# A two-layer decoder trunk on eight cores: the sample group transposed, its outer products in two row tiles, gMLP weights loaded transposed in bf16, first loads in turn

## The chip, the cores and the metric

The kernel runs on all 8 cores of one Trainium2 chip. Each core computes one prompt sequence of 2048 tokens and 16 of the 128 single-token samples; the cores do not exchange data. The metric is device time in microseconds (us) of the slowest core. Most executions agree closely: 17 of the 20 runs of the kernel before took 1262.70 to 1264.68 us. Some fall into a second, slower state: two or four cores of one die (four of the eight) show a lower granted clock (the share of TensorE's full clock that the trace records), and the time is longer.

PE is TensorE, DVE is VectorE, ACT is ScalarE, POOL is GpSimd, SP is SyncE, which here only issues DMA transfers.

## The reference, cut

```python
D_MODEL, BATCH, SEQ, DEPTH, DEC_BATCH, DEC_SEQ = 1024, 8, 2048, 2, 128, 1
# 8 retention heads and 8 gMLP heads of width 128, chunks of 128 tokens

def _layer(h, pos, S0, norm_g, w_in, w_out, ws, bs, ln_g, ln_b):
    xn = _rmsnorm(h, norm_g)
    q, k, v, g_r, u, v_g, g_g = split(xn @ w_in)            # 7 x 1024 columns
    q, k = rope(q), rope(k) * 128 ** -0.5
    o, S = _retention(q, k, v, S0)         # S_n = g S_{n-1} + k_n^T v_n ; o_n = q_n S_n
    o = o * rsqrt(mean(o * o) + EPS) * silu(g_r)            # per head
    vn = _layernorm(v_g, ln_g, ln_b)
    s = _spatial_gate(vn, ws, bs)          # s_i = sum_{j<=i} W[i,j] v_j + b_i, lower triangle
    m = u * s * silu(g_g)
    return h + concat(o, m) @ w_out, S, vn

def reference(...):
    for l in range(DEPTH):                 # prompt and sample share the weights
        h_p, S_p, _   = _layer(h_p, pos_p, zeros, ...)
        h_s, S_s, v_s = _layer(h_s, pos_s, state_ret[l], ...)
    return _rmsnorm(h_p), _rmsnorm(h_s), states_prompt, states_sample, vn_sample
```

For a sample of one token, the state update is one outer product of k and v per sample and head, and the spatial gate needs only the first element of each head's weight and bias.

## The kernel before

A list scheduler takes each operation with its reads, writes and an estimated duration, and orders the instructions of every engine. A layer runs in three stages: the v and v-gate projections of 16 chunks ("V stage"), 32 units of 8 heads and 4 token groups ("head stage"), and the output projection of 16 chunks ("out stage"). The sample's work is threaded through them.

The sample has its 16 rows on 16 partitions; its activations are the stationary operand, and the weights stream past, 512 columns at a time:

```python
        s_at = cur[0]
        stt = [T("stt%d" % i, [128, 8, 128], F32) for i in range(2)]     # sample states, 2 halves of 8
        ...
        xh_s = T("xh_s", [NS, D], F32, at=s_at)       # these five lie ON the state tiles
        lng_s = T("lng_s", [NS, D], F32, at=s_at + 4096)
        hs = T("hs", [NS, D], F32, at=s_at)           # (lnb_s, xs_s, fing_s cut)
        ...
        def s_mm(i):
            b = tbank()
            def mm(e):
                for k in range(8):
                    r = e.matmul(ps[0:NS, b, :], sxT[:, k, :], wv[i][:, k, :], start=(k == 0), stop=(k == 7))
                return r
            pe(mm, sxT.k() + wv[i].k(), [bk(b)], 8 * MM)
            return b
        ...
        def sample_vg(l, after=()):                   # LayerNorm of the sample's v-gate
            b0 = s_mm(2)
            b1 = s_mm(3)
            i = ln_stats(NS, b0, b1)
            # ... ACT normalises into xh_s; POOL: xh_s *= lng_s; POOL: xh_s += lnb_s (1024 columns each)
            pe(tr, xh_s.k() + identf.k(), [bk(b)], 8 * SM)      # 8 fp32 transposes
            # ... DVE: two passes into sT_s
        ...
        def w_prep(l, h):                             # gMLP weights: transpose, mask, sum of columns
            b = brot()
            pe(lambda e: e.transpose(ps[:, b, 0:128], ws_h[:], identf[:]), ws_h.k() + identf.k(), [bk(b)], 0.25)
            dve(lambda e: e.tensor_tensor(out=WTf[:], in0=ps[:, b, 0:128], in1=maskT[:], op=ALU.mult), ...)
            pool(lambda e: e.tensor_copy(WT[h % 2][:], WTf[:]), WTf.k(), WT[h % 2].k(), 128)
        def w_prep2(l, h):
            pe(lambda e: e.matmul(ps[:, b2, 0:128], ones_f[:], WTf[:], start=True, stop=True), ...)   # fp32
        ...
        def s_kv(l, h, half):                         # outer products k^T v of 8 samples, 4 to a matmul
            t = stt[half]
            for j in range(2):
                b = brot()
                pe((... e.matmul(ps[:, b, :], kn_s[:], vmask[:, j * 4:j * 4 + 4, :]...)), ..., [bk(b)], MM)
                # ... DVE: t = gamma * t + ps
```

`vmask` holds v of each sample in its own block of 128 columns and zero elsewhere, so one matmul with 16 rows makes four outer products. The first loads and the start of layer 0:

```python
        def x_load(l, c):
            xi[c] = dma("sp", hb[c % 4][:], src[c * 128:(c + 1) * 128, :], ...)     # a chunk of x, 512 KB
        ...
        for c in range(4):
            x_load(0, c)
            if c == 0:
                ld(identf, c_ident)
                ld(small, c_small, 51200)
                dma("sp", hs[:], xs_in, ...)
                w_item(0, ("v", 0))                   # first v weight: two loads on POOL's queue
        for l in range(DEPTH):
            if l == 0:
                for c in range(4):
                    norm_front(c); x_load(0, c + 4); norm_back(0, c, 1 + (c == 0))
                for n, (i, k) in enumerate(((1, 0), (1, 4), (2, 0), (2, 4), (3, 0), (3, 4))):
                    w_item(0, ("v", i, k), after=[xi[n + 2]])
                sample_norm(0)
            ...                                       # the V stage
            for half in range(2):
                s_load(l, 0, half)                    # states of head 0: stt[half], 512 KB each, on SP
```

## Time and profile before

| | before |
|---|---|
| time, median of 20 runs (fast about 1263) | 1263.73 us |
| mean granted TensorE clock, by core | 0.993 to 0.994 |
| PE busy | 1217.7 us, 96% |

The first lines are from the page of the kernel before, the profile of its slowest core: busy time, share of the span and number of instructions of each engine; then the engines' shares of the chain of work that ended last.

```profile
PE 1217.7 (96%) x7666; PEld 610.2 (48%) x7666; DVE 735.0 (58%) x1443; ACT 611.7 (48%) x1020; POOL 539.3 (43%) x536
...
PE 92%; DVE 3%; issue 2%; ACT 1%; DMA 1%; POOL 1%; SPq 0%; DVEq 0%; ACTq 0%; POOLq 0%
```

PE is busy almost throughout and is 92% of the chain. From this I expected that PE time taken away in a dense stretch comes off the total one for one (e13 below tests it), and that the other engines matter only where PE waits for them.

The next lines are the timeline of PE on core 3: start, duration, engine, line, output and inputs, partitions x columns, count; in brackets the idle time before and what ended it. Consecutive matmuls overlap in this view (a single one of 512 columns shows 0.379 us, yet eight take 1.73 from start to start), so costs are read from start to start.

```profile
8.29 1.01 PE L530 MATMUL ps<-identb,xs_105 128*128 128x128 bf16 x8 [8.29 <-DVE xs_105 L514]
...
19.95 1.01 PE L530 MATMUL ps<-identb,xs_106 128*128 128x128 bf16 x8 [4.97 <-DVE xs_106 L514]
...
33.34 1.89 PE L563 MATMUL ps<-wv_102,xnT 128*128 128x512 bf16 x8
...
57.06 1.89 PE L604 MATMUL ps<-wv_101,sxT 128*16 128x512 bf16 x8
58.79 1.89 PE L604 MATMUL ps<-wv_102,sxT 128*16 128x512 bf16 x8
60.61 1.90 PE L563 MATMUL ps<-wv_103,xnT 128*128 128x512 bf16 x8
...
103.11 5.30 PE L563 MATMUL ps<-wv_101,xnT 128*128 128x512 bf16 x16 [3.66 <-ACT VM L451]
...
191.01 0.60 PE L897 MATMUL ps<-vmask,kn_s 16*128 16x512 bf16 x2
191.54 0.49 PE L839 MATMUL ps<-WTf,ones_f 128*128 128x128 f32 x2
191.86 1.89 PE L658 MATMUL ps<-xnT,wsl_54 128*128 128x512 bf16 x8
...
229.12 1.89 PE L658 MATMUL ps<-xnT,wsl_61 128*128 128x512 bf16 x8
230.84 0.22 PE L773 MATMUL ps<-scT_89,VO 128*128 128x128 bf16 x1
```

First: transposes start at 8.29, but chunk 1's only at 19.95, and the second v weight (wv_102) is used at 33.34. Then the sample's v projection: 16 wide matmuls, 57.06 to 60.61, 3.55 us. At 103.11 PE had idled for 3.66 us, and the 16 matmuls that follow take 5.1 us instead of 3.5. Next, a pair of outer products takes 191.01 to 191.54, 0.53 us, and the fp32 column sum 0.32. The last two lines are eight projection matmuls, 1.72 us from start to start.

The issues of SP's queue on core 3 (SPq: start, time the queue was held, destination and source): chunks 0, 1, 2 and, once its normalisation frees a buffer, chunk 4.

```profile
1.06 0.38 SPq L461 DMA_DIRECT2D hb_50<-xp  x1
...
2.90 0.42 SPq L461 DMA_DIRECT2D hb_51<-xp  x1
3.37 0.95 SPq L461 DMA_DIRECT2D hb_52<-xp  x1
...
8.22 0.33 SPq L461 DMA_DIRECT2D hb_50<-xp  x1
```

And the timeline of DVE on core 3 just before the last two PE lines above. Note the order: the masking of the scores (scT, which PE's line 773 needs) runs ahead of the two B_k passes of the rotary embedding.

```profile
228.03 0.68 DVE L667 TENSOR_TENSOR A_k<-ps,rope_48 128x512 f32<-128x512 f32 x1
228.64 0.74 DVE L733 SCALAR_TENSOR_TENSOR scT_89<-ps,small,maskT 128x512 bf16<-128x512 f32 x1
229.41 0.69 DVE L671 TENSOR_TENSOR B_k<-ps,rope_48 64x512 f32<-64x512 f32 x1
230.11 0.68 DVE L672 TENSOR_TENSOR B_k<-ps,rope_48 64x512 f32<-64x512 f32 x1
```

The table below splits the time into stages, from starts in the PE timeline, mean of the eight cores of the profiled run: start of the program to the sample's v projection; the rest of layer 0's V stage; and so on; the last stage ends with the last matmul.

| us | start to sample v | rest of V, layer 0 | heads 0 | out 0 | V, layer 1 | heads 1 | out 1 |
|---|---|---|---|---|---|---|---|
| before | 56.7 | 102.2 | 360.2 | 127.9 | 120.4 | 364.1 | 120.4 |

### The profile page before, as it was taken

The numbers are of one execution on the slowest core, as the hardware profiler recorded it, in microseconds if no ns is written. First come the engines' busy times: TensorE is split into PE (matmuls) and PEld (weight loads), VectorE is DVE, ScalarE is ACT, GpSimd is POOL, SyncE is SP. The second block draws the span as 40 slices with busy tenths as digits, with TensorE's granted clock in tenths as the row PEclk, the third lists the DMA queues.
The fourth block names the chain that finished last, engine by engine and source line by source line (L and its number), as shares of the span: only waits on it lengthen the run. The fifth ranks groups of instructions, "written<-read, shape, count | busy, mean of one in ns | idle before, by whom it ended". The sixth has DMA issues, their size and how long they took to land.

```text
span 1262.4 us, 23383 instructions; the slowest of 8 cores (1258.4 to 1262.4 us)
## 1 busy us (share of the span) xinstructions
PE 1217.7 (96%) x7666; PEld 610.2 (48%) x7666; DVE 735.0 (58%) x1443; ACT 611.7 (48%) x1020; POOL 539.3 (43%) x536
## 2 busy tenths in 40 slices
PE   3998999999999999999999999999999999999997
PEld 1444455555555555444444444555555555544443
DVE  3464467776776767453443334776777767763333
ACT  3353346556566665422222434566665665753222
POOL 1002137667666766400000312667766766750000
PEclk9999999999999999999999999999999999999999
DMA  9726406225424523547650260325424523444433
GB/s 194 191 78 130 67 6 116 57 64 116 90 49 92 114 57 91 124 166 203 142 168 0 63 109 5 71 57 111 97 48 93 107 55 72 120 111 130 150 120 117
DMA packets 105687, 124.65 MB, mean 99 GB/s; under 512 B 5664, under 2 KB 79648, under 8 KB 105568
## 3 DMA queue, kind: packets, MB, share of 16 engines
q1 hardware_dynamic: 89440, 85.40, 22.3%
q0 software_dynamic: 16128, 37.76, 19.2%
q8 instruction: 64, 1.05, 0.3%
q14 instruction: 55, 0.45, 0.1%
HBM read 126.01 MB, written 34.87 MB: 127 GB/s over the span
## 4 chain that ended last, share of the span: by engine, by line
PE 92%; DVE 3%; issue 2%; ACT 1%; DMA 1%; POOL 1%; SPq 0%; DVEq 0%; ACTq 0%; POOLq 0%
PE ps L658 43%; PE ps L938 19%; PE ps L563 15%; PE ps L897 1%; PE ps L728 1%; PE ps L792 1%; PE ps L857 1%; PE ps L812 1%; PE ps L746 1%; PE ps L604 1%; PE ps L773 1%; PE ps L715 1%; DMA hb_51<-xp 1%; PE ps L776 1%; PE ps L530 1%
## 5 line engine op out<-in xcount | busy, mean ns | idle before, releaser
L451 ACT ACTIVATE B_q<-ps 64x512 f32<-64x512 f32 x128 | 75.8, 592 | 65.8 <-DVE A_q L683 57.7
L451 ACT ACT_TABLE_LOAD x65 | 83.4, 1283 | 48.4 <-DVE tt L794 46.4
L787 POOL TENSOR_TENSOR VO<-og,tt 128x512 bf16<-128x512 f32 x64 | 80.1, 1274 | 31.2 <-ACT tt L451 31.1
L674 POOL TENSOR_TENSOR kT_84<-A_k,B_k 128x512 bf16<-128x512 f32 x32 | 40.7, 1271 | 84.1 <-DVE B_k L672 84.1
L563 PE MATMUL ps<-wv_101,xnT 128*128 128x512 bf16 x256 | 62.4, 398 | 11.8 <-DVE xnT L535 7.8
L755 DVE SCALAR_TENSOR_TENSOR S_90<-S_90,ps 128x128 f32<-128x128 f32 x240 | 67.6, 282 | 6.9 <-PE ps L746 2.6
L451 ACT ACTIVATE tt<-tt 128x1024 f32<-128x1024 f32 x64 | 67.4, 1053 | 2.3 <-ACT tt L451 0.4
L889 POOL TENSOR_TENSOR vmask<-eye_137,v_s 16x1024 bf16<-16x1024 f32 x32 | 60.4, 1887 | 10.4 <-PE ps L897 9.8
L563 PE MATMUL ps<-wv_104,xnT 128*128 128x512 bf16 x256 | 61.1, 379 | 0.0
L563 PE MATMUL ps<-wv_103,xnT 128*128 128x512 bf16 x256 | 60.9, 379 | 0.2 <-ACT VM L451 0.2
L563 PE MATMUL ps<-wv_102,xnT 128*128 128x512 bf16 x256 | 57.4, 379 | 0.0
L576 DVE CAST VO<-ps 128x512 bf16<-128x512 f32 x32 | 21.8, 690 | 56.5 <-PE ps L563 56.5
L782 DVE TENSOR_TENSOR og<-ps,sgr_96 128x512 f32<-128x512 f32 x32 | 22.1, 691 | 53.2 <-ACT sq L451 53.2
L822 POOL TENSOR_TENSOR VM<-s_100,sgg_99 128x512 bf16<-128x512 f32 x32 | 36.9, 1153 | 37.1 <-DVE s_100 L816 30.5
L623 POOL TENSOR_TENSOR xh_s<-xh_s,lng_s 16x1024 f32<-16x1024 f32 x2 | 4.7, 2338 | 107.5 <-ACT xh_s L451 107.5
L451 ACT ACTIVATE sq<-ps 128x512 fp32r<-128x512 f32 x64 | 38.2, 597 | 24.9 <-PE ps L776 24.1
L782 DVE TENSOR_TENSOR og<-ps,sgr_97 128x512 f32<-128x512 f32 x32 | 22.1, 692 | 48.1 <-ACT sq L451 48.1
L535 DVE TENSOR_TENSOR xnT<-ps,small 128x1024 bf16<-128x1024 bf16 (+1 forms) x33 | 39.0, 1183 | 17.1 <-PE ps L530 12.4
L563 PEld LDWEIGHTS ps<-wv_101,xnT 128*128 128x128 bf16 x256 | 25.4, 101 | 43.5 <-issue 18.2
L674 POOL TENSOR_TENSOR kT_85<-A_k,B_k 128x512 bf16<-128x512 f32 x32 | 40.8, 1274 | 12.8 <-DVE B_k L672 12.7
L688 POOL TENSOR_TENSOR qT_82<-A_q,B_q 128x512 bf16<-128x512 f32 x32 | 40.7, 1271 | 4.7 <-POOL B_q L687 0.3
L688 POOL TENSOR_TENSOR qT_83<-A_q,B_q 128x512 bf16<-128x512 f32 x32 | 40.7, 1271 | 0.6
(343 smaller groups left out, 3035.6 us busy)
## 6 DMA issues: line engine op xcount, KB each, us to landing
stt_109<-st SPq DMA_DIRECT2D x16, 512.0 KB, 4.3
stt_108<-st SPq DMA_DIRECT2D x16, 512.0 KB, 7.3
ss_out<-stt_108 SPq DMA_DIRECT2D x16, 512.0 KB, 3.6
ss_out<-stt_109 SPq DMA_DIRECT2D x16, 512.0 KB, 6.5
hb_50<-xp SPq DMA_DIRECT2D x8, 512.0 KB, 4.8
hb_51<-xp SPq DMA_DIRECT2D x8, 512.0 KB, 5.5
hb_52<-xp SPq DMA_DIRECT2D x8, 512.0 KB, 7.3
hb_53<-xp SPq DMA_DIRECT2D x8, 512.0 KB, 5.7
```

The lines of the kernel that those rows point to most:

```text
L451: P.add("act", lambda e: e.activation(out=out, in_=in_, func=func, **kw), r, w, t_act(n) + (0.2 if "accum_out" in kw else 0), tset=tset)
L535: dve((lambda j: lambda e: e.tensor_tensor(out=xnT[:, j:j + m, c * 128:(c + 1) * 128], in0=pb.rearrange("p (k t) -> p k t", k=8)[:, j:j + ...
L563: r = e.matmul(ps[:, b, :], xnT[:, k, c * 128:(c + 1) * 128], wv[i][:, k, :], start=(k == 0), stop=(k == 7))
L658: r = e.matmul(ps[:, b, :], w[:, k, :], xnT[:, k, s], start=(k == 0), stop=(k == 7))
L674: pool(lambda e: e.tensor_tensor(out=dst[:], in0=A_k[:], in1=B_k[:], op=ALU.add), A_k.k() + B_k.k(), dst.k(), 512)
L688: pool(lambda e: e.tensor_tensor(out=dst[:], in0=A_q[:], in1=B_q[:], op=ALU.add), A_q.k() + B_q.k(), dst.k(), 512)
L755: return e.scalar_tensor_tensor(out=S32[:, c, :], in0=S32[:, (c + 3) % 4, :], scalar=_C["sdec"][h], in1=src, op0=ALU.mult, op1=ALU.add)
L782: dve(lambda e: e.tensor_tensor(out=og[:, u.n % 2, :], in0=ps[:, b, :], in1=g[:], op=ALU.mult), g.k(), og.k(u.n % 2) + [bk(b)], 512)
L787: pool(lambda e: e.tensor_tensor(out=VO[:, h, s], in0=og[:, u.n % 2, :], in1=tt[:, u.n % 2, :], op=ALU.mult), og.k(u.n % 2) + tt.k(u.n % 2 ...
L822: pool(lambda e: e.tensor_tensor(out=VM[:, h, qsl(u.q)], in0=s32[:], in1=g[:], op=ALU.mult), s32.k() + g.k(), VM.k(h, rng), 512)
L889: pool(lambda e: e.tensor_tensor(out=vmask[:], in0=eye16[:, half * 8:half * 8 + 8].unsqueeze(2).to_broadcast([NS, 8, 128]), in1=v_s[:, h * ...
L938: r = e.matmul(ps[0:n, banks[half], :], cat_fn(kk), w[:, k2, half * 512:(half + 1) * 512], start=(kk == 0), stop=(kk == 15))
```

## The change

The intent: give the sample's data all 128 partitions and make the weights stationary, so that its projections stream 16 columns instead of 512; put the k and v of the samples 4 to a group of 32 rows, so that the two outer-product matmuls of a pair use different row tiles (bands of 32 rows); let the host transpose the gMLP weights and load them as bf16; and issue the first loads in turn rather than all at once. The core of the diff, with cuts:

```diff
-        vmask = T("vmask", [NS, 8, 128], BF16)
-        xh_s = T("xh_s", [NS, D], F32, at=s_at)          # and the other tiles that lay on stt
+        vmask = T("vmask", [128, 4, 128], BF16)
+        hsT = T("hsT", [128, 8, NS], F32)                # tiles of their own
+        sA = T("sA", [128, 8, NS], F32)                  # sB, sC, sD likewise
 ...
         def s_mm(i):
-                for k in range(8):
-                    r = e.matmul(ps[0:NS, b, :], sxT[:, k, :], wv[i][:, k, :], start=(k == 0), stop=(k == 7))
+                for m in range(8):
+                    w = wv[i + m // 4]
+                    for k in range(8):
+                        r = e.matmul(ps[:, b, m * NS:(m + 1) * NS], w[:, k, (m % 4) * 128:(m % 4 + 1) * 128], sxT[:, k, :],
+                                     start=(k == 0), stop=(k == 7))
 ...   # sample_norm, sample_vg, s_gn: statistics by fp32 ones matmuls, short POOL passes of 128 columns
+        def s_rstd(src, scale):
+            pool(lambda e: e.tensor_tensor(out=sB[:], in0=src[:], in1=src[:], op=ALU.mult), src.k(), sB.k(), 128)
+            b = s_sum(sB)                                # DVE tensor_reduce, then PE ones_f x sC
+            act(... AF.Ln ...); act(... AF.Exp ...)
 ...
         def w_prep(l, h):
-            pe(lambda e: e.transpose(ps[:, b, 0:128], ws_h[:], identf[:]), ...)
-            dve(... WTf = ps * maskT ...); pool(... WT = copy of WTf ...)
+            pool(lambda e: e.tensor_tensor(out=w[:], in0=ws_h[:], in1=maskT[:], op=ALU.mult), ...)
         def w_prep2(l, h):
-            pe(lambda e: e.matmul(ps[:, b2, 0:128], ones_f[:], WTf[:], ...))
+            pe(lambda e: e.matmul(ps[:, b2, 0:128], ones_b[:], w[:], ...))
 ...
         def s_kv(l, h, half):
+            def mm(e):
+                for j in range(2):
+                    p0 = (half * 2 + j) * 32
+                    r = e.matmul(ps[:, bs[j], :], kn_s[p0:p0 + 32, :], vmask[p0:p0 + 32]..., start=True, stop=True)
+                return r
 ...
         def s_out(l):
-            o_mm(l, 0, banks, lambda k: catS[:, k, :], lambda k: catS.k(k), NS, range(8))   # 32 x 512 columns
+            for m0 in range(0, 8, 2): ...                # 128 matmuls of 16 columns
 ...
-        for c in range(4):
-            x_load(0, c)
-            if c == 0:
-                ld(identf, c_ident)
-                ...
-                w_item(0, ("v", 0))
+        x_load(0, 0)
+        ld(identf, c_ident)
+        ld(small, c_small, 55296)
+        dma("sp", hsT[:]..., xs_in, ...)
+        x_load(0, 1, "act")
+        va = w_item(0, ("v", 0, 0))
+        w_item(0, ("v", 0, 4), after=[xi[0]])
+        x_load(0, 2, "sp", after=[va])
+        x_load(0, 3, "act", after=[xi[1]])
```

## The prediction

> **What bounds the kernel now.** TensorE. The page gives PE 96% busy; the chain of waits is 92% PE. Idle PE time in the timeline lies in few places: the start (about 26 us lost up to 61 us, beside 128 matmuls at 0.216 us, transposes and sample work), a 3.65 us stall at 103.9 us followed by 8 matmuls at half rate, and waits up to 1.9 us elsewhere. The two long head stages run with almost no gap, so PE time removed there comes off the total one for one; DVE (58%), ACT (48%) and POOL (43%) only feed.
>
> **PE time removed or added** (start-to-start times from the timeline, both layers):
> - Sample v and vg projections: 64 moving passes of 512 columns, 3.65 us per 16, 14.6 us. After: 256 matmuls of 16 columns. The sample's head projections already have that form: 40 took 1.03 us, 0.0257 each. 6.6 us, plus transposes of v (16 x 0.056). Saves 7.1.
> - Sample output projection: 7.0 us per layer against 128 x 0.0257 = 3.3. Saves 7.4.
> - Outer products: a pair takes 0.54 us plus about 0.09 to enter. [...] no trace here shows it yet. If so each of 32 pairs loses one pass, 0.216 us: 6.9, plus 0.3 where pairs were split.
> - The transpose of k: with 16 columns it costs 0.30 us[...]; at full width 0.056 to 0.1. Saves 3.0.
> - gMLP weights: fp32 transpose 0.11 x 16 gone, fp32 column-sum matmul 0.32 to 0.06, x 16. Saves 6.0.
> - Sample transposes (0.29 and 0.57 per layer) gone: 1.7. New fp32 sums over partitions, about seven at 0.17, and the fp32 group norm: costs 1.5.
> Sum: about 31 us.
>
> **Waits.** The 3.65 us stall is the sample's LayerNorm: two POOL passes of 2.3 us hold up a transpose on PE, then DVE and the bn_stats behind it, then the PSUM banks. The new form has short POOL operations and nothing on DVE or PE behind the last of them. With smaller sample waits I expect 5 of some 8 us back. Each new chain (DVE, PE, ACT, POOL, DVE, PE) may stall a microsecond: 2 us against.
>
> **First loads.** x1 landed only at 16.7 us and the constants at 12.4, beside 2 MB of v weights and a head weight slice not needed until much later; DMA was 99% busy from 10 to 20 us. In turn, chunk 1 should start some 8 us earlier and the second v weight at about 27 instead of 33. Estimate: 6 us earlier in the steady stage.
>
> POOL also loses some 40 us of mask work, off the critical path: worth nothing.
>
> **Prediction:** 1264 - 31 - 3 - 6 = 1224 us; range 1211 to 1240. Faster by over 2%: 0.86; within: 0.13; slower: 0.01.
>
> **What would show it.** PE busy falls; sample matmuls of 16 columns 0.026 us apart; the two outer products of a pair start within some 10 ns; a pair takes about 0.33 us; the second v weight's first matmul near 27 us; no idle over 2 us at 90 to 110 us; head stages each some 9 us shorter.
>
> **What would make it wrong.** Row tiles that run in series (7 us back); a reordered instruction stream that puts a short sample chain in front of in-order PE (several us); loads in turn that leave DMA idle at the start; weight loads tied to projections that hold POOL.

The sum is 31 us (7.1 + 7.4 + 7.2 + 3.0 + 6.0 + 1.7 - 1.5 = 30.9). The cut under "Outer products" held the hypothesis to which "If so" refers, that the two matmuls of a pair run at once when they lie in different row tiles; e4 below tests it. Its 6.9 us is an estimate under this hypothesis, from 32 pairs and 0.216 us, the start-to-start time of a matmul of 512 columns. The 0.17 us of a new fp32 sum and the microsecond for each new chain were estimates; no trace had shown them.

## The result

| | before | after |
|---|---|---|
| median | 1263.73 us (20 runs) | 1233.11 us (10 runs, 1231.12 to 1234.96) |
| ratio of fast runs | | 0.976, 95% interval 0.9752 to 0.9769 |
| spans of the cores, profiled run | 1258.4 to 1262.4 | 1226.8 to 1233.4 |
| mean granted clock, by core | 0.993 to 0.994 | 0.989 to 0.991 |

A ratio is the mean time of one kernel's fast runs over that of the other's of the same rounds, so it is not quite the ratio of the medians. Executions in which one die ran at a lower clock are left out of the means. The kernel is 30.6 us faster and inside the predicted range, 9 us above the point. By stage:

| us | start to sample v | rest of V, layer 0 | heads 0 | out 0 | V, layer 1 | heads 1 | out 1 |
|---|---|---|---|---|---|---|---|
| before | 56.7 | 102.2 | 360.2 | 127.9 | 120.4 | 364.1 | 120.4 |
| after | 61.7 | 90.7 | 353.1 | 124.5 | 115.7 | 358.5 | 116.7 |
| difference | +5.0 | -11.5 | -7.1 | -3.4 | -4.7 | -5.6 | -3.7 |

Every stage but the first became shorter. The first, where 6 us should have been won, became 5 us longer. The lower mean clock has a place too: in stretches of 3.41 us, or multiples of it, the traces show half clock, and in the first stage this takes 3.2 us of clock from after (time x (1 - clock), mean of eight cores) and nothing from before. The page of the kernel after:

```profile
PE 1187.9 (96%) x8018; PEld 605.1 (49%) x8018; DVE 721.2 (58%) x1415; ACT 608.9 (49%) x1012; POOL 508.5 (41%) x560
...
PE 94%; DVE 2%; DMA 1%; issue 1%; ACT 1%; SPq 0%; DVEq 0%; POOL 0%; ACTq 0%; POOLq 0%
```

PE lost 29.8 us of busy time, about what the total lost, and its share of the chain rose to 94%. POOL lost 31 us, which is worth nothing here (it is 0% of the chain). The PE timeline of core 3, at the places shown for before:

```profile
19.83 1.01 PE L530 MATMUL ps<-identb,xs_105 128*128 128x128 bf16 x8 [19.83 <-DVE xs_105 L514]
...
32.40 1.01 PE L530 MATMUL ps<-identb,xs_105 128*128 128x128 bf16 x8 [3.54 <-DVE xs_105 L514]
...
44.22 6.15 PE L570 MATMUL ps<-wv_102,xnT 128*128 128x512 bf16 x26
...
65.34 0.96 PE L613 MATMUL ps<-sxT,wv_101 128*128 128x16 bf16 x32
66.15 0.95 PE L613 MATMUL ps<-sxT,wv_102 128*128 128x16 bf16 x32
66.96 1.02 PE L570 MATMUL ps<-wv_103,xnT 128*128 128x512 bf16 x4
...
188.11 0.39 PE L905 MATMUL ps<-vmask,kn_s 32*128 32x512 bf16 x2
188.43 0.23 PE L841 MATMUL ps<-WT_145,ones_b 128*128 128x128 bf16 x1
188.50 1.89 PE L662 MATMUL ps<-xnT,wsl_54 128*128 128x512 bf16 x8
...
225.31 1.89 PE L662 MATMUL ps<-xnT,wsl_61 128*128 128x512 bf16 x8
227.29 0.22 PE L777 MATMUL ps<-scT_89,VO 128*128 128x128 bf16 x1
```

The first transposes now start at 19.83 instead of 8.29, chunk 2's at 32.40, and the second v weight at 44.22 instead of 33.34 (38.4 to 44.2 over the cores; predicted 27). The 64 thin matmuls take 65.34 to 66.96, 1.62 us instead of 3.55, so 0.0253 each. The pair of outer products takes 0.32 us instead of 0.53, and the two are displayed as 0.39 us long, hardly longer than one (0.384): the second starts 3 to 4 ns after the first. The column sum takes 0.07. The stall near 104 us is gone; PE idles nowhere over 2 us between 90 and 110.

The last two lines show something not predicted. The eight projections before the score product take 1.98 us, where before showed 1.72.

SP's queue on core 3 shows what happened to the first loads:

```profile
1.07 0.39 SPq L460 DMA_DIRECT2D hb_50<-xp  x1
...
3.63 0.52 SPq L460 DMA_DIRECT2D stt_108<-st  x1
4.19 7.03 SPq L460 DMA_DIRECT2D stt_109<-st  x1
19.77 0.34 SPq L460 DMA_DIRECT2D hb_50<-xp  x1
20.20 0.38 SPq L460 DMA_DIRECT2D hb_52<-xp  x1
```

Two loads of the samples' states (stt), 512 KB each, come out right behind the small constants; the second holds the queue for 7 us. The next chunk (hb_50 is chunk 4) waits for chunk 0 to be normalised, and chunk 2 (hb_52), issued at 3.37 before, stands behind it until 20.20.

A late chunk 2 is passed on. The first half of the second v weight waits for its landing (`after=[xi[n + 2]]` in the code above): on core 3 it is issued at 30.01 us, where before issued it at 20.35. Over the eight cores chunk 2 landed at 18.9 us on average in before and at 25.9 in after, and the second weight was complete at 33.4 and 38.1.

And DVE on core 3, just before the score product:

```profile
223.95 0.68 DVE L671 TENSOR_TENSOR A_k<-ps,rope_48 128x512 f32<-128x512 f32 x1
...
224.86 0.69 DVE L675 TENSOR_TENSOR B_k<-ps,rope_48 64x512 f32<-64x512 f32 x1
225.56 0.68 DVE L676 TENSOR_TENSOR B_k<-ps,rope_48 64x512 f32<-64x512 f32 x1
226.28 0.75 DVE L737 SCALAR_TENSOR_TENSOR scT_89<-ps,small,maskT 128x512 bf16<-128x512 f32 x1
```

The B_k passes now run ahead of the masking of the scores, which starts at 226.28; PE wants its result at 227.04 and starts at 227.29.

### The profile page after: what moved, and what is told of

Same layout as the page of the kernel before. It is cut to its first block, busy times and chain, and to the rows that moved or that the text cites. A ratio compares the mean times of both kernels' runs of the same rounds, so it can differ in the third digit from the quotient of the medians.

```text
span 1233.4 us, 23892 instructions; the slowest of 8 cores (1226.8 to 1233.4 us)
## 1 busy us (share of the span) xinstructions
PE 1187.9 (96%) x8018; PEld 605.1 (49%) x8018; DVE 721.2 (58%) x1415; ACT 608.9 (49%) x1012; POOL 508.5 (41%) x560
## 3 DMA queue, kind: packets, MB, share of 16 engines
q0 software_dynamic: 18432, 38.28, 18.9%
q10 hardware_dynamic: 288, 1.05, 0.3%
## 4 chain that ended last, share of the span: by engine, by line
PE 94%; DVE 2%; DMA 1%; issue 1%; ACT 1%; SPq 0%; DVEq 0%; POOL 0%; ACTq 0%; POOLq 0%
PE ps L662 44%; PE ps L949 18%; PE ps L570 18%; PE ps L777 1%; PE ps L859 1%; PE ps L796 1%; DMA hsT<-xs 1%; PE ps L530 1%; PE ps L732 1%; PE ps L750 1%; PE ps L816 1%; PE ps L719 1%; PE ps L780 1%; PE ps L905 1%; PE ps L991 1%
## 5 line engine op out<-in xcount | busy, mean ns | idle before, releaser
L583 DVE CAST VO<-ps 128x512 bf16<-128x512 f32 x32 | 22.1, 692 | 61.7 <-PE ps L570 61.7
L894 POOL TENSOR_TENSOR vmask<-eye_137,v_s 128x512 bf16<-128x512 f32 x16 | 16.6, 1036 | 88.2 <-ACT v_s L450 88.1
L826 POOL TENSOR_TENSOR VM<-s_100,sgg_99 128x512 bf16<-128x512 f32 x32 | 37.0, 1156 | 25.9 <-DVE s_100 L820 12.3
L450 ACT ACTIVATE xs_105<-hb_50 128x1024 bf16<-128x1024 f32 x12 | 12.7, 1057 | 66.6 <-DVE hb_50 L968 52.4
L450 ACT ACTIVATE stb<-stt_109 128x1024 bf16<-128x1024 f32 x16 | 16.9, 1057 | 52.0 <-DVE stt_109 L910 52.0
L692 POOL TENSOR_TENSOR qT_82<-A_q,B_q 128x512 bf16<-128x512 f32 x32 | 40.6, 1270 | 3.3 <-POOL B_q L691 0.3
```

The costliest lines, as they stand in the source:

```text
L450: P.add("act", lambda e: e.activation(out=out, in_=in_, func=func, **kw), r, w, t_act(n) + (0.2 if "accum_out" in kw else 0), tset=tset)
L583: dve(lambda e: e.tensor_copy(o, src), [], wk, 512)
L692: pool(lambda e: e.tensor_tensor(out=dst[:], in0=A_q[:], in1=B_q[:], op=ALU.add), A_q.k() + B_q.k(), dst.k(), 512)
L826: pool(lambda e: e.tensor_tensor(out=VM[:, h, qsl(u.q)], in0=s32[:], in1=g[:], op=ALU.mult), s32.k() + g.k(), VM.k(h, rng), 512)
```

## The experiments

Twelve kernels were run, each against the kernel before in the same rounds. All gave correct results except e4_same_tile. After was measured in other rounds than they were, and they in three groups of rounds, so the ratios to before are the safer comparison.

### Why the start is late: e1_state_held, e2_norm_late, e3_both

My theory: two things that the diff does not announce. First, in before the sample's tiles lay on the state tiles, so the state loads had to wait until the sample's LayerNorm was done (some 95 us). With tiles of their own, nothing holds them, and the scheduler issues them at 3 us. Second, the new sample norm stands first in DVE's in-order queue: DVE's reduction waited until 18.66 us for POOL's square of hsT, whose load landed at about 18.1, and chunk 0's normalisation behind it ran only at 18.94 although its input had been ready since 10.8. The rival: the loads in turn are late by themselves.

e1 holds the first state loads of each layer until late in the V stage:

```diff
+                if p == 26:
+                    mark["st"] = mark["v"]
 ...
-                s_load(l, 0, half)
+                s_load(l, 0, half, after=[mark["st"]])
```

> The changed kernel, with one thing undone: the first two state loads of each layer (512 KB each) wait again for a v-gate matmul in the middle of the first stage, as the shared buffers made them wait before the change. Theory A (the state loads that went to the front take DMA time and block the SP queue, 4 to 7 us in issuing the second one, so the sample's input lands at 12 to 18 us and x2 is issued at 16 to 20 us): about 1228 us, 5 us off the changed kernel's 1233, the sample's input landing before 10 us. Theory B alone (the sample's norm in DVE's queue is what costs, whatever the loads do): at most 2 us off. Rival C (loading in turn itself leaves too little in flight): no change, 1232 to 1234.

e2 moves the sample's first norm to step 8 of the V stage:

```diff
-                sample_norm(0)
 ...
+                if p == 8 and l == 0:
+                    sample_norm(0, after=[mark["v"]])
```

> The changed kernel, with the sample's first RMS norm moved behind the eighth v chunk, so that its reduction no longer stands in DVE's queue ahead of chunk 0. State loads still at the front. Theory B: first transpose on PE near 10 us instead of 14 to 20, and x4 and x2, which stand behind it on the SP queue, issued some 4 us earlier: about 1229 us. Theory A alone: the loads keep their crowd, at most 2 us off 1233. Rival C: no change.

e3 does both.

> Both of the above. If A and B are each a part: 1222 to 1226 us, and the first v-gate matmul of layer 0 starts near 55 us instead of 61 to 67. If they are one and the same delay: no better than the better of the two. Rival C: 1232 to 1234.

| | median us | ratio, 95% | start to sample v | first PE work |
|---|---|---|---|---|
| after | 1233.11 | 0.976 (0.9752 to 0.9769) | 61.7 | 15.2 |
| e1_state_held | 1228.22 to 1233.31 (fast, 4 of 6) | 0.974 (0.9725 to 0.9754) | 58.9 | 14.9 |
| e2_norm_late | 1235.06 | 0.9773 (0.9761 to 0.9786) | 63.8 | 11.1 |
| e3_both | 1230.58 | 0.9739 (0.9726 to 0.9751) | 58.4 | 11.4 |

The last two columns are means of the eight cores of the profiled runs. The state loads cost about 3 us (e1 against after; the intervals just touch, and e3 against e2 shows more). The late first transposes do not matter by themselves: e2 starts PE 4 us earlier and is no faster. Its second weight is complete at 37.7 us, hardly before after's 38.1. Both fixes together still leave the start 1.7 us later than before. So the loads in turn, too, were on trial.

One part of the start was not followed up in the runs: the half clock. All nine kernels with the loads in turn lose clock in the first stage, 1.1 (e9) to 7.3 us (e2) on average over the cores; the five with the loads at once (before, e8, e10, e11, e13) lose none on any core. How much of this lengthens the start, and how much falls where PE waits for loads anyway, no run separates; in e2 it may be what took back the earlier start.

### Is the turn itself to blame: e6_turn_only, e8_at_once, e10_at_once_only

e6 is the kernel before with only the new order of the first loads.

> The kernel before, with one part of the change alone: the first loads in turn (x1 and x3 from ACT's queue, the second half of the first v weight after x0, x2 after the first half, x3 after x1). Its state loads are still held by shared buffers. My prediction gave this part 6 us: 1258. Theory D (the first 50 us are bound by what 16 DMA engines move, share about 1.0 and near 210 GB/s before and after; turning loads around within the first 4 MB doesn't bring the second v weight earlier): within 2 us of 1264, the second v weight's first matmul still at 32 us or later.

e8 is e3 with the first loads as in before; e10 is after with only that:

```diff
-        x_load(0, 1, "act")
-        va = w_item(0, ("v", 0, 0))
-        w_item(0, ("v", 0, 4), after=[xi[0]])
-        x_load(0, 2, "sp", after=[va])
-        x_load(0, 3, "act", after=[xi[1]])
+        for c in range(4):
+            x_load(0, c)
+            if c == 0:
+                ...                                  # constants and hsT as above
+                w_item(0, ("v", 0))
```

> The kernel with state loads held and the sample's norm late (1230.6), with the first loads as before the change: x0 to x3 on SP, the first v weight whole, nothing waiting. Theory D: the turn is worth nothing, 1229 to 1232 or even a little faster, since x2 comes no later. If the turn does help: 1234 or more.

> The kernel after with only the first loads put back as they were in the kernel before; the early state loads and the early sample norm stay. If the turn costs its 3.5 us whatever else is loaded (the difference of e3 and e8), about 1229.5 us, ratio 0.973, and the sample v projections start about 58 us instead of 61.7. If the turn's loss comes only from something in e3, or the turn protects chunk 1 from the state loads, 1233 or more. If the turn carries nearly all of the loss, the start falls to 56 and the time to 1227, as in e8, and the state loads and the norm would be innocent once the turn is gone.

| | median us | ratio, 95% | start to sample v |
|---|---|---|---|
| e6_turn_only | 1261.56 | 0.9982 (0.9956 to 1.0009) | 57.6 (before 56.7) |
| e8_at_once | 1227.03 | 0.9705 (0.9682 to 0.9728) | 55.9 |
| e10_at_once_only | 1228.46 | 0.9721 (0.9708 to 0.9733) | 57.8 |

On the kernel before, the turn gained nothing that is clear of the noise: the start is 0.9 us later, the rest of layer 0's V stage 4.6 us shorter (97.6), the first out stage 1.4 longer. Without it, the kernel is faster by 4.7 us with the state loads and the norm where the change put them (e10 against after) and by 3.6 us with both held back (e8 against e3); holding them seems worth another 1 to 2 us (start 55.9 in e8 against 57.8 in e10, total 1.4 us), but the two intervals overlap. e8's 0.9705 is a better kernel than after. The turn was meant to win 6 us and lost some 4.

### Which part of the turn: e9_need_order, e12_x2_free

e9 (on e3) chains sixteen first loads strictly in the order of need, each waiting for the one two places before it, with the constants first on ACT's queue:

```diff
+        def turn(kind, *a):
+            af = [ch[-2]] if len(ch) >= 2 else []
+            ...                                      # issue with after=af, append to ch
+        for it in (("x", 0), ("v", 0, 0), ("x", 1), ("v", 0, 4), ("x", 2), ("x", 3), ("v", 1, 0), ("v", 1, 4)):
+            turn(*it)
```

> The same kernel (state held, norm late) with all of the first 16 loads in the order of need (x0, half v weight, x1, half, x2, x3, second v weight, x4 to x7, v-gate weights), each waiting for the one two places before it, and the constants first on ACT's queue. If theory D holds, the same bytes in this order bring the second v weight in at about 25 us instead of 35, and the first v-gate matmul at about 50 us instead of 60: 1220 to 1225. If two loads at a time leave the DMA engines idle, their share falls below 0.9 and the time stays at 1230 or rises.

It took 1231.4 us, ratio 0.974 (0.9714 to 0.9765), as e3. Its sample projection starts at 52.6 us, but with less done by then, and the rest of the V stage takes 98.3 us instead of 90.5: the DMA share fell to 0.69 on average from 10 to 40 us, and the last three of the four halves of the v-gate weights were issued at 45 to 61 us (on core 3 of e3 at 26 to 36). A strict chain leaves the queues partly empty; what is gained early is paid later.

e12 (on e3) undoes one word of the turn, the wait of chunk 2 for the first half weight:

```diff
-        x_load(0, 2, "sp", after=[va])
+        x_load(0, 2, "sp")
```

> e3 (turn kept, state loads held, norm late), with chunk 2's load no longer held behind the first half weight. If the loss of the turn is chunk 2's late place in the in-order queue, which also delays the second weight: the second v weight's first matmul 3 us earlier and 1228 us. If it is chunk 1 on the second queue[...]: first PE work still at 11 us, and 1230.6 us as e3.

It took 1225.80 us (1224.75 to 1227.43), ratio 0.9702 (0.9689 to 0.9714), and its sample projection starts at 54.6 us, 3.8 earlier than e3's. The chain of waits of e3, core 3, in order of time (start, length, what):

```profile
1.58 10.95 DMA wv<-w_v
...
12.60 9.60 DMA hb<-xp
```

The first half weight takes from 1.58 to 12.53; only then, at 12.60, is chunk 2 issued, and it lands at 22.20. SP's queue of e12 on core 3 (consecutive issues merged into one line: start of the first, stretch up to the last, and their number):

```profile
2.91 34.71 SPq L460 DMA_DIRECT2D hb<-xp  x9
```

Here chunk 2 is the first of the nine, at 2.91. (In after, on this core, it was issued even later, at 20.20, because the scheduler had put it behind chunk 4, which waits for chunk 0's normalisation.) First PE work stays at 11.1 us (e3 11.4) and chunk 1 stays on ACT's queue, so that place, the rival, is not what cost the time. The wait did let other loads land sooner: over the cores, the second half of the first weight at 18.5 us in e3 and 20.7 in e12, chunk 3 at 15.9 and 20.3. But chunk 2 came at 21.5 and 17.7, and the second weight, chained to it, was complete at 35.0 and 31.7: about what the start gained. What e12 undoes is the wait together with the place in the queue: in e3, too, chunk 2 stood behind chunk 4 (issued at 12.14 on core 3), and without the wait the scheduler put it in front. These two are not separated. In e6 chunk 2 landed at 23.1 and the second weight was complete at 37.5, yet the start is 57.6, so the link is not the whole story. The gain was larger than either theory said. With this wait gone and the state loads held, the start is 2.1 us earlier than before.

### Do the two products of a pair run at once: e4_same_tile

Both matmuls of a pair are put into the same group of 32 rows; the sample's states are then wrong.

```diff
-                    p0 = (half * 2 + j) * 32
+                    p0 = half * 64
```

> The changed kernel, wrong on purpose: both outer products of a pair read the same 32 partitions, so they are in the same row tile[...]. Everything else is equal. If the pair runs concurrently in the changed kernel (0.32 us with the entry and exit), each of 32 pairs should take 0.22 us longer, and the whole 7 us: about 1240. If row tiles gave nothing, no change.

It took 1240.75 us, ratio 0.9821 (0.9808 to 0.9833), 7.6 us more than after (one slow run left out). The PE timeline of core 3:

```profile
197.03 0.60 PE L905 MATMUL ps<-vmask,kn_s 32*128 32x512 bf16 x2
197.56 1.90 PE L662 MATMUL ps<-xnT,wsl 128*128 128x512 bf16 x8
```

The pair takes 0.53 us from start to start, as in before, instead of 0.32, although both operands have 32 rows in both kernels. Only the row tile differs, so this confirms that the pair runs concurrently in after: the second of a pair starts 3 to 4 ns after the first in after and 0.226 us after it in e4, and 32 pairs x 0.21 us is 6.7 us of the 7.6.

### A half clock after 128 thin matmuls: e5_spread, e11_spread_best

The windows of core 3 of after around the sample's output projection in layer 0 (stretch; length; busy time and count of PE, PEld, DVE, ACT, POOL; granted clock; DMA share; GB/s):

```profile
577.00:580.60 3.60, 3.60 (x138) 3.60 (x136) 2.42 (x3) 0.87 (x1) 0.00 (x0) 1.00 1.02 305
580.60:584.30 3.70, 3.70 (x15) 1.38 (x13) 1.32 (x3) 0.78 (x4) 0.39 (x1) 0.54 0.35 106
```

The 128 matmuls of 16 columns from 577.34 to 580.58 keep PE 100% busy, yet the following 3.7 us run at clock 0.54. Six of eight cores show this, losing some 1.7 us each; cores 0 and 5 do not, nor does any core in layer 1, where the same 128 matmuls run. Core 0, the run and what follows it:

```profile
572.80:576.10 3.30, 3.30 (x133) 3.30 (x131) 2.27 (x3) 0.88 (x1) 0.00 (x0) 1.00 1.00 334
576.10:579.70 3.60, 3.60 (x24) 1.80 (x21) 1.32 (x3) 1.26 (x6) 0.40 (x1) 1.00 0.65 199
```

My theory: the unbroken run of thin matmuls brings on the half clock; by what mechanism, no run shows. e5 cuts the run into four pieces of 32 behind four different chunks:

```diff
-                if c == 8:
-                    s_out(l)
+                if c in (6, 7, 8, 9):
+                    s_out_part(l, 2 * (c - 6))       # 32 matmuls, a bank and an add of its own
+                if c == 9:
+                    s_out(l)
```

> The changed kernel, its sample output projection cut into four pieces of 32 matmuls, each behind another output chunk (6 to 9), each with its own bank and sum. Theory H (3.3 us of nothing but 16-column matmuls lets the granted clock fall to half: in layer 0 it was 0.54 to 0.57 for 3.7 us after them on six of eight cores): the clock stays at 1.0 after each piece on every core and those cores gain about 1.7 us; the kernel 1 to 2 us faster, 1231 to 1232. Rival (the fall is chance, or comes from the DMA share of 1.0 in that stretch): the clock falls there as before, 1233.

e11 does the same on e8.

> e8 (first loads at once, state loads held, sample norm late) with the sample's output projection cut in four pieces as in e5. If the half clock after 128 thin matmuls in a row costs about 1.5 us and the two fixes add up: 1225.5 us, ratio 0.9695, clock 1.0 from 540 to 600 us on all cores, the first output stage about 1.5 us and the second about 0.9 us shorter than e8's 124.7 and 116.6. If the pieces only move the loss elsewhere: 1227, as e8.

| | median us | ratio, 95% | out 0 | out 1 | clock lost, 540 to 600 us |
|---|---|---|---|---|---|
| after | 1233.11 | 0.976 | 124.5 | 116.7 | 1.7 us on 6 cores |
| e5_spread | 1232.25 to 1233.19 (fast, 3 of 7) | 0.9752 (0.9718 to 0.9787) | 123.2 | 115.8 | 0 on all |
| e8_at_once | 1227.03 | 0.9705 (0.9682 to 0.9728) | 124.7 | 116.6 | 1.7 us on 7 cores |
| e11_spread_best | 1225.99 | 0.9702 (0.9689 to 0.9714) | 123.4 | 115.8 | 0 on all |

In both pairs the half clock is gone and the out stages are shorter by about 1.3 and 0.9 us. The 1.3 fits what was lost (1.7 us on 6 of 8 cores is 1.3); the 0.9 is something else, since no core of after or e8 lost clock after the run in layer 1. In the total, one microsecond is within the intervals, so the total neither confirms nor denies it. e5's start happened to be 1.6 us later than after's, which swallowed the gain.

The kept traces also settle the rival and say which cores lose. Within each core's trace, all changes of the clock lie on one grid of 3.413 us. Nine kernels have the run in one piece (3.2 us): 144 runs with both layers and all cores. All 48 that start from 0.40 us before to 0.48 us after a point of the grid are followed by half clock; none of the 96 others is, which start from 0.50 us after one point to 0.49 before the next. The DMA share during the run, in layer 0, is 0.94 to 1.05 with the loss and 0.94 to 1.04 without, so DMA does not decide it. In these traces the run costs clock when it nearly fills one stretch of the grid; in layer 1 it did so on 2 of 72 occasions.

### The gMLP part alone: e13_gmlp_only

The head stages should each have become some 9 us shorter and became 7.1 and 5.6. e13 is the kernel before with only the gMLP weights transposed on the host, loaded as bf16 on POOL's queue, masked in one step and summed in bf16 (the edit is the w_prep, w_prep2 and load hunks of the change).

> The kernel before, with only the gMLP weights loaded transposed in bf16, masked in one step and summed in bf16 (loads held behind the projections as in the change). The prediction's term for this part: 16 transposes of 0.11 us and 16 sums 0.25 us shorter, 6.0 us in all: 1257.7 us, ratio 0.9953, each head stage 3 us shorter (360.2 and 364.1 before). If the gain is partly hidden or the converting load gets in the way of the head weights: 1260 or more.

Result: 1261.99 to 1264.28 us in the three fast runs of six, ratio 0.9996 (0.9978 to 1.0014). Nothing was gained. The table divides the head stages into start-to-start time by kind of matmul, mean of eight cores:

| us, layer 0 + layer 1 | before | e13 | after |
|---|---|---|---|
| fp32 transposes of gMLP weights | 1.14 + 1.21 | 0 | 0 |
| column sums | 2.28 + 2.27 | 0.64 + 0.46 | 0.59 + 0.46 |
| outer products | 10.31 + 10.25 | 10.37 + 10.37 | 6.67 + 6.67 |
| transposes of k | 1.30 + 1.24 | 1.30 + 1.31 | 0.50 + 0.50 |
| projections of 512 columns | 270.00 + 271.26 | 271.53 + 272.65 | 272.39 + 273.16 |
| whole stage | 360.2 + 364.1 | 359.2 + 364.9 | 353.1 + 358.5 |

The removed work is as large as predicted: 5.8 us of gMLP matmuls in e13. But the projections, which nobody touched, take 2.9 us longer in e13 and 4.3 in after. On core 3, once in 14 of the 16 heads of e13 and of after, one group of eight before the score product takes 1.97 us or more instead of 1.73; in before, in two of sixteen. The DVE timeline of e13, core 3, shows the order seen in after:

```profile
230.93 0.68 DVE L673 TENSOR_TENSOR B_k<-ps,rope 64x512 f32<-64x512 f32 x1
231.64 0.75 DVE L734 SCALAR_TENSOR_TENSOR scT<-ps,small,maskT 128x512 bf16<-128x512 f32 x1
```

With the masking of the gMLP weights gone from DVE, the scheduler chose another order there: two B_k passes of 0.7 us each, ahead of the masking of the scores that PE waits for. About 0.24 us in 12 more heads makes 2.9 us, and on core 3 such groups lose 4.0 us in all in e13 and 3.7 in after, against 0.5 in before. The rest went elsewhere: e13's start is 0.9 us later, and PE's idle time in layer 1's head stage rose from 4.9 to 5.9 us. No run put the masking first again, so that the order of DVE causes the waits is not shown by undoing it. But before holds both orders itself. Its two heads with the long group are the last of each layer, in which no weights of a next head are left to mask; there the B_k passes run first:

```profile
497.95 0.69 DVE L671 TENSOR_TENSOR B_k<-ps,rope_48 64x512 f32<-64x512 f32 x1
498.66 0.68 DVE L672 TENSOR_TENSOR B_k<-ps,rope_48 64x512 f32<-64x512 f32 x1
499.38 0.75 DVE L733 SCALAR_TENSOR_TENSOR scT_89<-ps,small,maskT 128x512 bf16<-128x512 f32 x1
```

And in the first head of each layer of e13 and after the masking still runs first, and the group takes 1.73 us. In all three kernels, on cores 3 and 6, every long group has the B_k passes just before the masking, and none with the masking first is long (two or three groups with the B_k passes first are not long either).

## Why the prediction was right or wrong

The prediction was 1224 us (1211 to 1240); the result, 1233.11, lies in the range. By term:

| term | predicted | measured |
|---|---|---|
| PE work removed and added | -31 | about -27: the work went as costed, some 4 us came back as waits, most of them in the head stages |
| waits of the sample's chains | -3 | about -9 |
| first loads | -6 | +5.0 |
| sum | -40 | -31 |

The measured rows come from the stage table: heads -12.7 where 16.2 were predicted; out -7.1 where 7.4 were; the two V stages together -16.2, of which about 7.3 is the predicted PE work (7.1 + 1.7 - 1.5) and the rest, 9, is waits by subtraction; start +5.0. That the sum came within 9 us is partly luck: 6 us more from waits than predicted offset part of the 11 us lost on the loads.

- **The mis-sized step is "First loads ... Estimate: 6 us earlier in the steady stage"**: 11 us off, and in sign. The prediction argued from a list of transfers with a late landing, not from queues. It missed the wait of chunk 2 for a transfer of 11 us, in an in-order queue (3.8 us with the place in the queue that it brought, e12 against e3), and the 1 MB of state loads that moved to the front because their buffers were no longer shared (about 3 us, e1). Both were in the diff, the second only as a change of addresses. "In turn" also freed no bandwidth: in the timeline the DMA share is 0.9 or more in most slices from 5 to 50 us, before and after (core 3, mean of 0 to 50 us: 0.95 and 202 GB/s before, 0.93 and 205 GB/s after).
- **Thin projections**: right. 64 took 1.62 us against 1.65 predicted; 128 took 3.24 against 3.3.
- **Row tiles**: right, and the hypothesis that no trace showed is confirmed by e4, 7.6 us where 6.9 + 0.3 had been estimated. Entering a pair took about 0.10 us in after: the 128-column matmul before a pair takes 0.152 us from start to start, those before it 0.056.
- **Transpose of k**: right. Over the eight heads of a layer the step went from 1.30 (layer 1: 1.24) to 0.50 us, and the product just before it from 1.19 to 0.45: together 3.0 us in both layers, as predicted. One such step with the product just before it took 0.30 us at 16 columns in before and takes 0.11 at full width in after; what the longer one spends its time on was not shown.
- **gMLP weights**: the PE time is right (5.8 of 6.0), the claim that it "comes off the total one for one" is wrong. Alone it gave nothing (e13), because removing a DVE operation reordered DVE. The head stages were called dense, but the masking of the scores had little in hand: on core 3 it ended 1.46 us before PE used it in before, and two B_k passes ahead of it take 1.4 us.
- **Waits**: right in cause, too small in size. The stall of 3.65 to 4.04 us, a wait of 0.85 before it and the half clock after it (2.6 us of clock, mean of the cores) went entirely: some 7 of the 9 us. The stall also hangs on the loads: in e6, with the sample's old chains and the loads in turn, it is 2.1 to 2.3 us and no half clock follows. e10, with the new chains and the old loads, has 90.7 us in this stage as after does, so the chains alone remove it. The fear of new stalls from the sample's longer chains was nearly idle: the v-gate chain cost one wait of about 0.5 us in layer 1, and on core 0 one of 0.69 in layer 0.
- **What would make it wrong**: the list named "a reordered instruction stream that puts a short sample chain in front", and that occurred, on DVE (first transposes at 15.2 instead of 8.0 us on average). e2, which undoes it, was no faster.

The best kernels measured are e12_x2_free (1225.80) and e11_spread_best (1225.99). e12 with the spread projection was not run.

What stays open: why spreading does not clearly show in the total; whether putting the mask first on DVE returns the 3 us; how much of the start the half clock there costs; and how much of the remaining startup is bound by DMA alone.

## What to carry to other kernels

When tiles are moved to addresses of their own, ask which transfers their sharing held back: those will now be issued early, in the busiest stretch (here two loads of 512 KB moved from about 95 us to 3 us, which cost about 3 us, e1 against after). A wait on a transfer, in an in-order queue, puts it behind whatever the queue itself waits for (here chunk 2 behind chunk 4, issued at 20.20 us in after instead of 3.37 in before); hold a load back only if what lands sooner for it is what the engine waits for, and look what else is chained to the load. And with a scheduler, work taken from PE pays only if the order of the feeding engine stays good (in e13 5.8 us of PE work went and nothing was gained): compare start-to-start times of the untouched groups before and after, since there the loss appears.
